# A hybrid attention block: the head norm's input is copied out of its bank by ScalarE, and scaled in SBUF by VectorE

## The chip, the core and the metric

One core of one Trainium2 chip runs the whole program. The metric is the device time of one launch in microseconds (us). The kernel before was timed in three runs: median 1075.9 us, lowest 1073.9, highest 1076.67. The execution that was profiled took 1073.98 us; its span, from the first instruction of the program to the last, is 1071.9 us, so 2.1 us lie around the span.

## The reference

One decoder layer over 512 real tokens and 16 meta tokens of width 1024, in float32: a SwiGLU feed-forward block, a token mixer with two attention branches and output gates, and a second feed-forward block. The change lies in the token mixer, where queries and keys of both branches pass through a norm over each head of 64 features:

```python
def rms_norm(x, g):
    xf = x.astype(jnp.float32)
    ms = jnp.mean(xf * xf, axis=-1, keepdims=True)
    return (xf * lax.rsqrt(ms + EPS) * g.astype(jnp.float32)).astype(x.dtype)

    proj = h @ w_in                       # h is the token's own rms_norm, 1024 wide
    qa = rms_norm(qa.reshape(b, p, FOX_HEADS, HEAD_DIM), fox_q_norm)
    ka = rms_norm(ka.reshape(b, p, FOX_HEADS, HEAD_DIM), fox_k_norm)
    ...
    qb = rms_norm(qb.reshape(b, p, SWA_Q_HEADS, HEAD_DIM), swa_q_norm)
    kb = rms_norm(kb.reshape(b, p, SWA_KV_HEADS, HEAD_DIM), swa_k_norm)
```

The forgetting branch (8 heads, all earlier tokens visible) and the sliding-window branch (8 query heads over 2 key heads, 128 tokens visible and the meta tokens) then compute scores, softmax and values.

## The kernel before

Every product runs as three fp32r products: each operand is split into a high part (`hi`, a copy on ScalarE, line 133 or 134) and a low part (`lo`, a subtraction on VectorE, line 140 or 142), and `prod` (lines 301, 302 and 304) multiplies high by high, high by low and low by high. Weights go the same way: the DMA lands in a tile `raw`, ScalarE writes `wh`, VectorE writes `wl`.

The mixer projects one tile of tokens at a time (128 tokens, or the 16 meta tokens, which are tile 0) against 256 columns of weights. `tok_chunk` makes two steps of each tile, with 12 matmuls each, and hands the finished bank to `evac`. For query and key columns `evac` calls `head_norm`: ScalarE squares the bank into a tile `hsq` (line 1057), VectorE sums each head into `hss` (line 1058) and applies the token's own mean square (`r1sq`, line 1059), and GpSimd raises it to the power -0.5 (line 351, in place). `head_norm` returns a function `scale`, which is called only when the next tile has been evacuated. It multiplies the bank by the token's factor `r1` and by the head's factor `hss` on VectorE (line 1073) and writes `qn`. So the bank of a tile is held from its first matmul until the scaling, one tile later. Tiles `qn` come from a pool of six. When all tiles of a chunk are there, `finish` transposes `qn` on TensorE (line 1153, 1161 or, for the sliding keys, 1407) and splits the result into `qH`, `qL`, `kH` and `kL`.

There are eight PSUM banks, four by the name `ps` and four by the name `pt`; in the mixer they are taken in turn, one of each name. All users share them: projections, transposes, scores and values.

The projection steps are woven between the steps of attention units (`weave`): a unit has `scores` (matmuls at line 1292, VectorE's addition and minimum at line 1310, exponentials at line 1209, normalisation at line 1212), `turn` (transposes at lines 1337 and 1350, split into `pH` and `pL`) and `values` (lines 1359, 1364 and 1365). A scheduler then sets the order of each engine's queue from the program order, the dependences and its own estimate of durations; this order is fixed when the program is built, and each engine works through its queue in that order. Scores of two heads use 64 of the 128 rows of TensorE each, one head the upper half and one the lower half, in a `ps` bank and a `pt` bank.

Of the kernel before, what the change touches and what calls it, by code (L numbers as in the profile page):

```python
# [13 lines left out]
AF = mybir.ActivationFunctionType  # L14
ALU = mybir.AluOpType
# [29 lines left out]
def bc(ap, pos, n):  # L45

    dims = [list(d) for d in ap.ap]
    dims.insert(pos, [0, n])
    return bass.AP(tensor=ap.tensor, offset=ap.offset, ap=dims)
# [33 lines left out]
def kernel(  # L83
# [22 lines left out]
    V, A, G, PE, SP = nc.vector, nc.scalar, nc.gpsimd, nc.tensor, nc.sync  # L106
# [9 lines left out]
    def nm(s):  # L116
        nid[0] += 1
        return f"{s}_{nid[0]}"
# [231 lines left out]
    def rsq(o, i):  # L350
        shared["pow"] = G.tensor_tensor(out=o, in0=i, in1=nhalf[: i.shape[0], : i.shape[1]], op=ALU.pow)
# [106 lines left out]
    class Units:  # L458
# [5 lines left out]
        def new(self, tag, bufs, w=1):  # L464
            return self.pool.tile([P, w * self.th], F32, tag=tag, name=nm(tag), bufs=bufs)
# [522 lines left out]
    r1 = cp.tile([P, NB + 1], F32, name="r1")  # L988
# [63 lines left out]
    def head_norm(ps, i, nh, outs):  # L1052

        n = M if i == 0 else P
        sq = new("hsq", [P, 256], F32, 3)
        ss = mp.tile([P, 4], F32, tag="hss", name=nm("hss"), bufs=4)[:n, :nh]
        A.activation(sq[:n, : nh * HD], ps[:n, : nh * HD], AF.Square)
        V.tensor_reduce(out=ss, in_=sq[:n, : nh * HD].rearrange("p (h d) -> p h d", d=HD), axis=AX.X, op=ALU.add)
        ts = V.tensor_scalar(ss, ss, r1sq[:n, i : i + 1], EPS, op0=ALU.mult, op1=ALU.add)
        shared["ts"] = getattr(ts, "ins", ts)  # L1060
        rsq(ss, ss)
        src, by = ps[:n, : nh * HD].rearrange("p (h d) -> p h d", d=HD), bc(ss, 2, HD)

        def scale():

            with tc.issue_after(shared["ts"]):
                r = r1[:n, i : i + 1]
                for o in outs:
                    a, b = src, by
                    if isinstance(o, tuple):  # L1070
                        o, par = o
                        a, b = (v.rearrange("p (a b) d -> p a b d", b=2)[:, :, par] for v in (src, by))
                    V.scalar_tensor_tensor(out=o, in0=a, scalar=r, in1=b, op0=ALU.mult, op1=ALU.mult)

        return scale

# [43 lines left out]
    def qk_chunk(box, tag, tiles, gcol):  # L1120
# [11 lines left out]
        def evac(i, ps):  # L1132
            n = M if i == 0 else P
            want = [0] if i == 0 else [i] if off else range(1, NB + 1)
            for j in want:
                if j not in qn:
                    qn[j] = new("qn", [P, 4, HD], F32, 6)
            if i == 0:
                G.memset(qn[i], 0.0)
            if off or i == 0:  # L1140
                return head_norm(ps, i, 4, [qn[i][:n]])
            pairs = lambda j: qn[j].rearrange("p (a b) d -> p a b d", b=2)
            return head_norm(ps, i, 4, [(pairs(i)[:, :, 0], 0), (pairs(NB + 1 - i)[:, :, 1], 1)])
# [231 lines left out]
    def kv_chunk(box):  # L1375
# [10 lines left out]
        def evac(i, ps):  # L1386
            n = M if i == 0 else P
            kd[i] = new("qn", [P, 2, 2, HD], F32, 6)
            if i == 0:
                G.memset(kd[i], 0.0)  # L1390
            scale = head_norm(ps, i, 2, [kd[i][:n, :, r] for r in range(2)])
            v_evac(box["v"][:, :, :256], i, ps[:n, P : 2 * P])
            return scale
# [140 lines left out]
    for i in every:  # L1534
        n = M if i == 0 else P
        ps = tok_result(ps0[i], i, 264)
        V.scalar_tensor_tensor(
            out=zf[:n, i], in0=ps[:, 256:264], scalar=r1[:n, i : i + 1], in1=fb[:n], op0=ALU.mult, op1=ALU.add
# [218 lines left out]
    src = {name: tuple([xS[name][:, p, k] for k in range(4)] for p in range(2)) for name in xS}  # L1757
# [78 lines left out]
    for i, step in enumerate(GATES):  # L1836
# [4 lines left out]
        b, m = step  # L1841
# [193 lines left out]
```

## Time and profile before

| what | value |
|---|---|
| median of three runs | 1075.9 us |
| profiled execution, its span | 1073.98 us, 1071.9 us |
| TensorE busy over the span | 1062.0 us (99%) |
| VectorE, ScalarE, GpSimd busy | 893.3 (83%), 652.8 (61%), 211.8 us (20%) |
| granted TensorE clock | 0.999 |
| scalings of line 1073 | 44, first at 386.9 us, last at 531.3 us |

In the rows, PE is TensorE, PEld its weight loads, DVE VectorE, ACT ScalarE, POOL GpSimd and SP SyncE. A row of grouped instructions gives line, engine, operation, output and inputs, shape, count, then busy us and mean ns of one, then the idle time of the engine just before them with what ended most of it. A row of the timeline gives start us, duration us, engine, line, operation, names, shape and count, and in brackets the idle time before it. Matmuls overlap, so the distance from one start to the next says more than a matmul's own duration.

### The profile page before, as it was taken

To read this page: it belongs to the slowest core of one execution; us is meant where nothing else is said; L and a number is where in the kernel's file an instruction comes from. 1 tells how busy PE (TensorE), PEld (TensorE's weight loads), DVE (VectorE), ACT (ScalarE), POOL (GpSimd) and SP (SyncE) were. 2 spreads that over 40 slices of the span, in tenths; PEclk is the share of its full clock that TensorE was granted. 3 is DMA by queue.
4 is the path that set the end of the run, shared out by engine and by line. 5 is a ranking of instruction groups with operands and counts; after the bars stand their busy time and mean duration, and the time that the engine had idled before them with its cause. 6 is when DMAs were issued, how large, how long until landed. Compare 5 with 4: busy or idle time off the path is not lost.

```text
span 1071.9 us, 22258 instructions
## 1 busy us (share of the span) xinstructions
PE 1062.0 (99%) x8515; PEld 1029.7 (96%) x8515; DVE 893.3 (83%) x1732; ACT 652.8 (61%) x1231; POOL 211.8 (20%) x281
## 2 busy tenths in 40 slices
PE   9999999999999999999999999999999999999998
PEld 8999999999999999999878799999999999999998
DVE  7988878888889678789897899888989788887895
ACT  7667456656666455556667776555665466745664
POOL 3011111121124432232200110001122211221120
PEclk9999999999999999999999999999999999999999
DMA  8787787688776413212311874566688877897763
GB/s 282 196 224 162 189 193 196 152 220 217 173 179 179 125 64 124 75 62 68 95 60 40 242 191 119 187 202 196 172 204 182 186 188 179 177 199 193 159 126 102
DMA packets 112571, 173.57 MB, mean 162 GB/s; under 512 B 10881, under 2 KB 59265, under 8 KB 112209
## 3 DMA queue, kind: packets, MB, share of 16 engines
q1 hardware_dynamic: 74464, 122.72, 36.4%
q0 software_dynamic: 29040, 37.83, 22.8%
q10 hardware_dynamic: 8960, 11.60, 3.3%
q8 instruction: 66, 1.08, 0.4%
q14 instruction: 41, 0.33, 0.1%
HBM read 167.89 MB, written 6.32 MB: 163 GB/s over the span
## 4 chain that ended last, share of the span: by engine, by line
PE 50%; DVE 3%; ACT 2%; issue 0%; DMA 0%; POOL 0%; ACTq 0%; DVEq 0%; POOLq 0%
PE ps L301 8%; PE ps L304 8%; PE ps L302 8%; PE pt L301 7%; PE pt L302 7%; PE pt L304 7%; ACT t L1209 1%; DVE wl L140 1%; ACT wh L133 1%; DVE pL L140 1%; PE ps L1473 0%; PE ps L1950 0%; PE pt L1473 0%; DMA raw<-in_wbr_dram 0%; DVE t L1212 0%
## 5 line engine op out<-in xcount | busy, mean ns | idle before, releaser
L301 PE MATMUL ps<-x,wh 128*128 128x256 f32 (+2 forms) x768 | 219.8, 286 | 0.2
L302 PE MATMUL ps<-x,wh 128*128 128x256 f32 (+2 forms) x768 | 218.9, 285 | 0.5 <-DVE x L142 0.4
L304 PE MATMUL ps<-x,wl 128*128 128x256 f32 (+2 forms) x768 | 218.8, 285 | 0.0
L140 DVE TENSOR_TENSOR wl<-raw,wh 128x1024 fp32r<-128x1024 f32 (+3 forms) x125 | 149.9, 1200 | 39.3 <-ACT wh L133 38.6
L133 ACT CAST wh<-raw 128x1024 fp32r<-128x1024 f32 (+3 forms) x125 | 128.4, 1029 | 85.7 <-PE ps L302 44.1
L301 PEld LDWEIGHTS ps<-x,wh 128*128 128x128 f32 x768 | 144.7, 189 | 1.8 <-ACT hT L686 0.3
L302 PEld LDWEIGHTS ps<-x,wh 128*128 128x128 f32 x768 | 144.5, 188 | 1.4 <-DVE x L142 0.9
L304 PEld LDWEIGHTS ps<-x,wl 128*128 128x128 f32 x768 | 144.7, 188 | 0.8
L301 PE MATMUL pt<-x,wh 128*128 128x256 f32 (+2 forms) x424 | 125.3, 296 | 0.0
L304 PE MATMUL pt<-x,wl 128*128 128x256 f32 (+2 forms) x424 | 124.6, 295 | 0.0
L302 PE MATMUL pt<-x,wh 128*128 128x256 f32 (+2 forms) x392 | 112.5, 287 | 0.0
L133 ACT CAST wh<-tc 128x1024 fp32r<-128x1024 f32 (+1 forms) x70 | 71.8, 1026 | 65.5 <-DVE tc L234 58.1
L140 DVE TENSOR_TENSOR wl<-tc,wh 128x1024 fp32r<-128x1024 f32 (+1 forms) x70 | 83.5, 1193 | 33.3 <-ACT wh L133 33.1
L301 PE MATMUL ps<-acts,wh 128*128 128x264 f32 (+1 forms) x352 | 100.5, 286 | 0.1
L304 PE MATMUL ps<-acts,wl 128*128 128x264 f32 (+1 forms) x352 | 99.8, 283 | 0.0
L302 PE MATMUL ps<-acts,wh 128*128 128x264 f32 (+1 forms) x352 | 99.6, 283 | 0.0
L140 DVE TENSOR_TENSOR wl<-rawC,wh 128x1024 fp32r<-128x1024 f32 (+1 forms) x70 | 84.2, 1202 | 5.7 <-ACT wh L133 5.2
L133 ACT CAST wh<-rawC 128x1024 fp32r<-128x1024 f32 (+1 forms) x70 | 71.5, 1022 | 22.8 <-PE pt L302 16.7
L301 PEld LDWEIGHTS pt<-x,wh 128*128 128x128 f32 x424 | 80.0, 189 | 2.3 <-ACT wh L133 0.2
L304 PEld LDWEIGHTS pt<-x,wl 128*128 128x128 f32 x424 | 79.8, 188 | 2.1
L302 PEld LDWEIGHTS pt<-x,wh 128*128 128x128 f32 x392 | 73.7, 188 | 0.6
L301 PEld LDWEIGHTS ps<-acts,wh 128*128 128x128 f32 x352 | 66.4, 189 | 0.7 <-DVE h2T L918 0.3
(446 smaller groups left out, 3236.5 us busy)
## 6 DMA issues: line engine op xcount, KB each, us to landing
rawC<-in_w1i_dram SPq DMA_DIRECT2D x20, 512.0 KB, 4.5
raw<-in_w1i_dram SPq DMA_DIRECT2D x40, 256.0 KB, 4.1
raw<-in_w2i_dram SPq DMA_DIRECT2D x40, 256.0 KB, 3.5
rawC<-in_w2i_dram SPq DMA_DIRECT2D x20, 512.0 KB, 4.3
raw<-in_wm_dram SPq DMA_DIRECT2D x18, 512.0 KB, 4.3
raw<-in_wout_dram SPq DMA_DIRECT2D x16, 512.0 KB, 4.0
rawD<-in_w1i_dram SPq DMA_DIRECT2D x20, 256.0 KB, 4.2
raw<-in_w1i_dram POOLq DMA_DIRECT2D x20, 256.0 KB, 5.4
```

The lines of the kernel that those rows point to most:

```text
L133: return A.copy(o, i)
L140: return V.tensor_tensor(out=o, in0=i, in1=h, op=ALU.subtract)
L301: PE.matmul(ps, sH, mH, start=first, stop=False, **more)
L302: PE.matmul(ps, sH, mL, start=False, stop=False, **more)
L304: shared["mm"] = PE.matmul(ps, sL, mH, start=False, stop=last, **more)
L1209: shared["exp"] = A.activation(t, t, AF.Exp, bias=nmx, scale=-1.0, accum_out=l[:, j : j + 1])
```

## The change

`head_norm` lets ScalarE copy the projected tile out of its bank, multiplied by the token's factor `r1`, right behind the square. The copy goes to the tile `qn` itself (for the sliding keys, to the first of its two places; for the forgetting keys, where the even and the odd heads go to two tiles, it is two copies of half the columns). `scale` then multiplies `qn` by the head's factor in place with a tensor-tensor operation; the second place of the sliding keys is written first, from the copy.

```diff
         src, by = ps[:n, : nh * HD].rearrange("p (h d) -> p h d", d=HD), bc(ss, 2, HD)
+        kept, todo = None, []
+        for o in outs:
+            a, b = src, by
+            if isinstance(o, tuple):
+                o, par = o
+                a, b = (v.rearrange("p (a b) d -> p a b d", b=2)[:, :, par] for v in (src, by))
+                kept = None
+            if kept is None:
+                kept = o
+                A.activation(kept, a, AF.Identity, scale=r1[:n, i : i + 1])
+            todo.append((o, kept, b))
 
         def scale():
 
             with tc.issue_after(shared["ts"]):
-                r = r1[:n, i : i + 1]
-                for o in outs:
-                    a, b = src, by
-                    if isinstance(o, tuple):
-                        o, par = o
-                        a, b = (v.rearrange("p (a b) d -> p a b d", b=2)[:, :, par] for v in (src, by))
-                    V.scalar_tensor_tensor(out=o, in0=a, scalar=r, in1=b, op0=ALU.mult, op1=ALU.mult)
+                for o, a, b in reversed(todo):
+                    V.tensor_tensor(out=o, in0=a, in1=b, op=ALU.mult)
```

The queues differ as follows. Line numbers behind line 1070 are six higher in the changed kernel.

ScalarE, in the first key chunk of the forgetting branch, behind the last load of an activation table; `hsq` is the square, `qn` the copy, `wh` the high part of a weight piece. Before:

```order
L1057 ACTIVATE hsq_5139<-ps_5110 128x256
L1057 ACTIVATE hsq_5171<-pt_5146 128x256
L1057 ACTIVATE hsq_5204<-ps_5179 128x256
L133 CAST wh_5076<-raw_4905 128x1024
L1057 ACTIVATE hsq_5237<-pt_5212 128x256
```

Now:

```order
L1057 ACTIVATE hsq_5140<-ps_5111 128x256
L1072 ACTIVATE qn_5136<-ps_5111,r_4883 128x2x64
L1072 ACTIVATE qn_5139<-ps_5111,r_4883 128x2x64
L1057 ACTIVATE hsq_5174<-pt_5149 128x256
L1072 ACTIVATE qn_5137<-pt_5149,r_4883 128x2x64
L1072 ACTIVATE qn_5138<-pt_5149,r_4883 128x2x64
L1057 ACTIVATE hsq_5209<-ps_5184 128x256
L1072 ACTIVATE qn_5138<-ps_5184,r_4883 128x2x64
L1072 ACTIVATE qn_5137<-ps_5184,r_4883 128x2x64
L133 CAST wh_5076<-raw_4905 128x1024
```

Each square is followed by its copies; the weight cast stands behind six of them.

TensorE, at the scores of an attention unit in the middle of the mixer, behind the transposes of the second key chunk (`kH`, `kL`, `qH` are split keys and queries; the 128x256 blocks of two heads go to a `ps` and a `pt` bank). Before:

```order
L1292 MATMUL ps_6171<-kH_5068,qH_5245 128x256
L1292 MATMUL ps_6179<-kH_5068,qH_5245 128x272
L1292 MATMUL ps_6179<-kL_5069,qH_5245 128x272
L1292 MATMUL ps_6179<-kH_5068,qH_5245 128x272
L301 MATMUL pt_6096<-wh_5759,x_4306 128x256
L302 MATMUL pt_6096<-wl_5760,x_4306 128x256
L304 MATMUL pt_6096<-wh_5759,x_4310 128x256
L301 MATMUL pt_6096<-wh_5759,x_4306 128x256
L1292 MATMUL pt_6172<-kH_5068,qH_5245 128x256
L1292 MATMUL pt_6172<-kL_5069,qH_5245 128x256
L1292 MATMUL pt_6172<-kH_5068,qH_5245 128x256
L302 MATMUL pt_6096<-wl_5760,x_4306 128x256
```

Now:

```order
L1167 MATMUL pt_6171<-ident,qn_5815 128x128 x2
L1298 MATMUL ps_6194<-kH_5068,qH_5254 128x256
L1298 MATMUL pt_6195<-kH_5068,qH_5254 128x256
L1298 MATMUL ps_6194<-kL_5069,qH_5254 128x256
L1298 MATMUL pt_6195<-kL_5069,qH_5254 128x256
L1298 MATMUL ps_6194<-kH_5068,qH_5254 128x256
L1298 MATMUL pt_6195<-kH_5068,qH_5254 128x256
```

The three matmuls of the second head no longer stand alone among projection matmuls; they alternate with those of the first head. The same happens once more, at the scores of the unit behind which the sliding keys are transposed.

TensorE, at the values of a later unit (`pv` is the `pt` bank, `pL` the low part of the probabilities). Before:

```order
L1364 MATMUL pt_6560<-pH_6530,v_4889 128x256
L301 MATMUL ps_6569<-wh_6043,x_4304 128x256
L302 MATMUL ps_6569<-wl_6044,x_4304 128x256
L304 MATMUL ps_6569<-wh_6043,x_4308 128x256
L301 MATMUL ps_6569<-wh_6043,x_4304 128x256
L302 MATMUL ps_6569<-wl_6044,x_4304 128x256
L1365 MATMUL pt_6560<-pL_6531,v_4889 128x256
```

Now:

```order
L1370 MATMUL pt_6589<-pH_6558,v_4889 128x256
L301 MATMUL ps_6598<-wh_6065,x_4304 128x256
L302 MATMUL ps_6598<-wl_6066,x_4304 128x256
L1371 MATMUL pt_6589<-pL_6559,v_4889 128x256
L1370 MATMUL pt_6589<-pH_6558,v_4889 128x128
L1371 MATMUL pt_6589<-pL_6559,v_4889 128x128
L304 MATMUL ps_6598<-wh_6065,x_4308 128x256
```

The matmul that reads `pL` stands three projection matmuls further forward. At two later units it stands one further forward, at an earlier unit two, and at one unit three further back.

## The prediction

> **What bounds the kernel now.** I read three views first: busy time by engine, then two stretches of 160 us side by side (a piece of the feed-forward block, and the piece of the mixer in which all 44 scalings lie), then the waits of TensorE. Columns of the stretches are length, busy us of PE, PEld, DVE, ACT and POOL with counts, granted clock, DMA share, GB/s.
>
> ```profile
> PE 1062.0 (99%) x8515; PEld 1029.7 (96%) x8515; DVE 893.3 (83%) x1732; ACT 652.8 (61%) x1231; POOL 211.8 (20%) x281
> ```
>
> ```profile
> 100.00:260.00 160.00, 159.98 (x1313) 159.66 (x1312) 131.45 (x221) 90.68 (x155) 29.38 (x34) 1.00 0.80 194
> 380.00:540.00 160.00, 157.38 (x1291) 147.40 (x1290) 131.37 (x392) 94.77 (x227) 46.91 (x92) 1.00 0.26 81
> 480.00:500.00 20.00, 19.76 (x168) 18.66 (x169) 18.45 (x61) 13.10 (x37) 4.81 (x13) 1.00 0.30 83
> ```
>
> ```profile
> PE pt L1365 <- DVE pL L140: 0.9, 3, 0.4
> PE ps L1292 <- DVE qn L1073: 0.5, 1, 0.5
> ...
> PE pt L1350 <- DVE qn L1073: 0.2, 1, 0.2
> ```
>
> TensorE is busy 99% of the span, at full clock. In the feed-forward stretch it idles for 0.02 us of 160; in the mixer stretch for 160 - 157.38 = 2.62 us. That is the whole reservoir of waits that this edit can empty, apart from matmuls that could stand better. 0.3% of 1075.9 us, about what a measurement of this kernel can tell from no change, is 3.2 us. VectorE is the engine that TensorE waits for: it is busy 82% of the mixer stretch and 18.45 of the worst 20 us, and the waits name its `pL` and its `qn`. ScalarE is busy 59% there, but the split of the probabilities, the exponentials and the weight casts all pass through it.
>
> **What the edit removes and adds.** The view of line 1073 counts the scalings, and the groups of the mixer give durations:
>
> ```profile
> L1073 DVE SCALAR_TENSOR_TENSOR qn<-ps,r,hss x22: 333/349/483, 388.3 to 531.3; 128x128 f32<-128x128 f32 x12, 128x256 f32<-128x256 f32 x10
> L1073 DVE SCALAR_TENSOR_TENSOR qn<-pt,r,hss x18: 332/347/484, 389.4 to 528.3; 128x128 f32<-128x128 f32 x12, 128x256 f32<-128x256 f32 x6
> L1073 DVE SCALAR_TENSOR_TENSOR qn<-hsq,r,hss x4: 332/399/473, 386.9 to 476.0; 16x256 f32<-16x256 f32 x2, 16x128 f32<-16x128 f32 x2
> ```
>
> ```profile
> L1106 DVE TENSOR_TENSOR oA<-pt,hsq 64x256 f32<-64x256 f32 x20 | 8.4, 420 | 2.2 <-ACT hsq L1105 1.8
> L1073 DVE SCALAR_TENSOR_TENSOR qn<-ps,r,hss 128x256 f32<-128x256 f32 x10 | 4.7, 474 | 0.0
> L1736 DVE SCALAR_TENSOR_TENSOR spare<-xg,gT,spare 128x256 f32<-128x256 f32 x4 | 1.7, 479 | 0.0
> ```
>
> The new operation, a tensor-tensor of 256 columns, has its nearest row in `oA`: 420 ns. The old one took 474, and the same operation with all its tensors in SBUF took 479. So leaving the bank gains VectorE nothing by itself; losing the scalar operand gains 0.05 to 0.06 us. 44 x 0.06 = 2.6 us of VectorE over the stretch. The bounds are 0 (no gain) and 2.6 us. Where it counts is ahead of a late `pL`: the view of waits has three at line 1365, and two scalings stand shortly before such a `pL` in VectorE's queue. I take **0.4 us** (3 x 2 x 0.06).
>
> [...]
>
> ScalarE gains 39 copies: 16 of 256 columns (queries), 20 of 128 (16 forgetting keys, 4 sliding keys), 3 of the meta tile.
>
> ```profile
> L134 ACT ACTIVATE v<-pt,r 128x256 fp32r<-128x256 f32 x5 | 2.4, 471 | 0.0
> ...
> L134 ACT ACTIVATE v<-ps,r 128x128 fp32r<-128x128 f32 x2 | 0.7, 362 | 0.0
> ```
>
> ```profile
> 491.52 0.38 ACT L1057 ACTIVATE hsq<-ps 128x256 f32<-128x256 f32 x1 [0.58 <-PE ps L304]
> 491.80 0.37 ACT L133 CAST pH<-ps 128x256 fp32r<-128x256 f32 x1
> ```
>
> The `v` rows are the same operation with the same scalar, 0.47 and 0.36 us. From the two timeline rows, the next instruction starts 0.10 us before the end of the last (491.80 against 491.90), so a copy holds up its queue by 0.37 or 0.26 us: 16 x 0.37 + 20 x 0.26 + 3 x 0.35 = **12.2 us** of ScalarE. This is the price of the edit, and the bounds are 0 and 12.2 us. Behind a copy stand, by turns, a probability cast (as at 491.80), a weight cast, an exponential or the next square. ScalarE idles 65 of the 160 us, and in the changed queue the exponentials and one probability cast stand ahead of the square that they followed. The cover is this idle time; where it is gone, `pH` is late, then `pL`, then line 1365. A copy waits for what its square has waited for (and for a free `qn`, whose transposes stand more than a tile earlier). I take **0.5 us**: two sites where a copy stands straight before a late cast.
>
> **What the bank's release gives.** Two waits name the scaling although the waiting matmul reads no `qn`: scores at line 1292 and probabilities at line 1350. They wait for the bank.
>
> ```profile
> 435.86 0.35 PE L1292 MATMUL ps<-kH,qH 64*128 64x256 f32 x1 [0.55 <-DVE qn L1073]
> ```
>
> ```profile
> 480.09 0.52 PE L1350 MATMUL pt<-ident,t 128*128 128x128 f32 x3 [0.24 <-DVE qn L1073]
> ```
>
> The copy releases the bank a tile earlier, so both go: **0.8 us** (0.55 + 0.24). What is late next there is VectorE's own `pL` and `t`, which are not in these rows; the bounds are 0 and 0.8.
>
> **What the moved matmuls give.** Scores of two heads that alternate run side by side; alone, each set of three pays for itself and for both changes of shape.
>
> ```profile
> 481.37 0.38 PE L1292 MATMUL ps<-kH,qH 64*128 64x256 f32 x1
> 481.37 0.38 PE L1292 MATMUL pt<-kH,qH 64*128 64x256 f32 x1
> ...
> 482.30 0.39 PE L301 MATMUL ps<-wh,x 128*128 128x256 f32 x1
> ```
>
> ```profile
> 452.04 0.28 PE L301 MATMUL pt<-wh,x 128*128 128x256 f32 x1
> 452.25 0.38 PE L1292 MATMUL pt<-kH,qH 64*128 64x256 f32 x1
> 452.47 0.28 PE L1292 MATMUL pt<-kL,qH 64*128 64x256 f32 x1
> 452.59 0.27 PE L1292 MATMUL pt<-kH,qH 64*128 64x256 f32 x1
> 452.79 0.39 PE L302 MATMUL pt<-wl,x 128*128 128x256 f32 x1
> ```
>
> ```profile
> 495.73 0.38 PE L1292 MATMUL ps<-kH,qH 64*128 64x256 f32 x1
> ...
> 496.28 0.44 PE L1407 MATMUL pt<-ident,qn 128*128 128x128 f32 x2
> ```
>
> Both heads start together at 481.37, and twelve matmuls are through in 0.93 us. The lone set at 452.25 stretches the step from one projection matmul to the next from 0.12 (452.47 to 452.59 shows the step of such a stream) to 0.75 us: 0.63 lost. The lone set at 495.73 costs 0.55. In the new order both run inside their partner's time. I take **1.1 us**; bounds 0, if the second bank is still late and the pair waits together, and 1.2.
>
> Against it stand the matmuls on `pL` that come further forward.
>
> ```profile
> 477.16 0.39 PE L1365 MATMUL pt<-pL,v 128*128 128x256 f32 x1 [0.31 <-DVE pL L140]
> ```
>
> This one already waits for VectorE, and three projection matmuls of 0.12 us now stand behind it: 0.36 us more. Two others stand one matmul further forward, 0.12 each at most. **0.6 us** lost in all; the bounds are 0, where VectorE is early enough, and 0.6. The one that moves back and the earlier one that moves forward I count at nothing: the three waits of that row are elsewhere.
>
> **Sum.** -0.4 - 0.8 - 1.1 + 0.5 + 0.6 = **-1.2 us**. Against the profiled execution's own 1073.98 us (its span of 1071.9 and 2.1 around it) that is 1072.8; that execution was 1.9 us under the median, so as a median I forecast 1075.9 - 1.2 = **1074.7 us**, no measurable change.
>
> **The rivals.**
>
> *ScalarE's queue gets in the way (slower).* Place: the probability casts and exponentials in 430 to 535 us, where a copy is queued ahead of them. The other terms give -1.7 us without the 0.5. So the kernel is slower by over 3.2 us if 4.9 of the 12.2 us, 40%, reach TensorE; at half (6.1) the time is 1075.9 - 1.7 + 6.1 = 1080.3. For it: each `pL` and `wl` of VectorE needs ScalarE's half first. Against it: ScalarE idles 41%, the square at 491.52 had 0.58 us of idle time ahead of it, and the waits quoted name VectorE alone. Chance 0.12.
>
> *The two-input scaling collides with GpSimd.* The scaling now reads two tensors in SBUF while GpSimd raises `hss` to its power there.
>
> ```profile
> L351 POOL TENSOR_TENSOR hss<-hss,nhalf 128x4 f32<-128x4 f32 x24 | 25.9, 1080 | 41.4 <-DVE hss L1059 41.4
> ```
>
> GpSimd is busy 46.91 of 160 us, 29%. If a scaling that meets it waits for half a power (0.54 us), that is 44 x 0.29 x 0.54 = 6.9 us of VectorE. A third of it on the path would be 2.3 us: 1077.0; all of it, 1081.6. Against it: VectorE's weight split has both inputs in SBUF too, and in the mixer, where GpSimd is busier (46.91 against 29.38), it took only 1236 ns against 1200 over the program:
>
> ```profile
> L140 DVE TENSOR_TENSOR wl<-raw,wh 128x1024 fp32r<-128x1024 f32 x29 | 35.9, 1236 | 4.0 <-ACT wh L133 4.0
> ```
>
> ```profile
> L140 DVE TENSOR_TENSOR wl<-raw,wh 128x1024 fp32r<-128x1024 f32 (+3 forms) x125 | 149.9, 1200 | 39.3 <-ACT wh L133 38.6
> ```
>
> Chance 0.05. [...]
>
> *The banks were the hidden limit (faster).* If the early release takes away all of the mixer's idle time, 2.6 us, with the 1.1 us of paired scores and half of the 0.4, the time is 1075.9 - 3.9 = 1072.0. For it: eight banks shared by all. Against it: only 0.8 us of the waits name the scaling. Chance 0.15.
>
> *Nothing moves.* The released banks wait for the next late thing, and the pairs run no earlier: 1075.9. Chance 0.10.
>
> **How the numbers follow.** My forecast has 0.58. Of it 0.56 lies within 0.3% and 0.02 below. The first rival is slower with all its 0.12; the second gives 0.02 to slower and 0.03 to the same; the third 0.13 to faster and 0.02 to the same; the last 0.09 to the same and 0.01 to slower. Faster 0.15, same 0.70, slower 0.15. The range reaches down to all gains at their bounds (2.6 + 0.8 + 1.2 - 0.6 = 4.0 us, with no copy on the path) less 0.7 us for the spread of a median, 1071.2, and up to a third of the copies' 12.2 us on the path (1075.9 - 1.7 + 4.1), 1078.3.
>
> **What would show it.** Right: the waits of lines 1292 and 1350 for `qn` are gone; the new tensor-tensor takes 0.41 to 0.43 us at 256 columns and the copies 0.46 to 0.48; twelve matmuls at line 1298 alternate where three stood alone; TensorE's idle time in the mixer stretch falls from 2.6 to about 1.8 us, with the wait at 477 us grown. Wrong: new waits of TensorE for `pH`, or for `pL` behind a ScalarE that was never idle; a tensor-tensor of over 0.5 us; or a bank that stays late although the copy is done, because something else holds it.

## The result, and the profile after

In 22 runs each, the changed kernel takes **1073.66 us** (1072.82 to 1075.08) and the kernel before 1075.23 us (1073.9 to 1077.24): a ratio of 0.9986, with a 95% interval of 0.9981 to 0.9992. The change gains 1.57 us, 0.15%. The forecast was -1.2 us and 1074.7 us.

The profiled execution of the changed kernel has a span of 1071.2 us (before 1071.9). First the busy time by engine, then the same 160 us of the mixer as before, with the same columns, then the waits of TensorE in the mixer (total us, times, longest).

```profile
PE 1060.0 (99%) x8515; PEld 1028.1 (96%) x8515; DVE 891.8 (83%) x1732; ACT 666.4 (62%) x1270; POOL 212.9 (20%) x281
```

```profile
380.00:540.00 160.00, 156.93 (x1299) 147.46 (x1298) 131.32 (x394) 107.57 (x268) 47.89 (x92) 1.00 0.26 81
```

```profile
PE pt L1371 <- DVE pL L140: 1.6, 4, 0.7
PE ps L1370 <- ACT pH L133: 0.3, 1, 0.3
PE ps L1413 <- DVE nmx L1316: 0.3, 1, 0.3
PE ps L1159 <- DVE qn L1079: 0.3, 1, 0.3
PE ps L302 <- DVE wl L140: 0.2, 1, 0.2
```

(Lines behind the edit are six higher than before: 1371 was 1365, 1298 was 1292.) The two waits for the bank are gone. In their place stand more waits for `pL`, and one each for `pH`, `nmx`, the transposes' `qn` and a weight piece `wl`. TensorE idles 160 - 156.93 = 3.07 us in this window, more than the 2.62 before, and yet eight more matmuls lie in it.

The operations came out close to the rows that stood for them. The groups of the mixer, shapes apart:

```profile
L1079 DVE TENSOR_TENSOR qn<-qn,hss 128x256 f32<-128x256 f32 x16 | 6.7, 418 | 2.0 <-POOL hss L351 2.0
L1079 DVE TENSOR_TENSOR qn<-qn,hss 128x128 f32<-128x128 f32 x24 | 6.2, 285 | 0.4 <-POOL hss L351 0.3
L1072 ACT ACTIVATE qn<-ps,r 128x256 f32<-128x256 f32 x10 | 4.7, 470 | 0.0
L1072 ACT ACTIVATE qn<-ps,r 128x128 f32<-128x128 f32 x10 | 3.3, 377 | 0.0
```

**Where the time went.** Busy shares don't answer that here, so I made a ledger: the matmuls of each trace are numbered by their start, 8515 in each kernel, and the start of the same number is compared with that in the kernel before. The difference at the mixer's first scalings (389 us) is taken off, since it is -0.58 to +1.31 us in these profiles and arises in the first block, where the kernels are alike. What is left is the gain (-) or loss (+) of each stretch, in us; the stretches are named by the times of the kernel before. Each ledger rests on one profile, and inside a group of matmuls whose order has changed the same number can be another matmul. But a step with the same cause comes out alike: nine of the kernels below and here have -0.90 or -0.92 us at 433 to 437 us.

| kernel | 389-433 | 433-437 | 437-448 | 448-457 | 457-476 | 476-487 | 487-494 | 494-497 | 497-507 | 507-518 | 518-531 | 531-562 | sum |
|---|---|---|---|---|---|---|---|---|---|---|---|---|---|
| changed | -0.05 | -0.90 | +0.07 | -1.08 | +0.24 | -0.38 | +0.25 | -0.23 | +0.54 | +0.50 | +0.01 | -0.29 | -1.32 |

So the change wins 2.9 us in five places and gives 1.6 us back in five others. The wins come first (436 to 482 us); most of the losses come at 490 to 515 us.

### The profile page after: what moved, and what is told of

The parts are those of the page before. It is cut to its first block, busy times and chain, and to the rows that moved or that the text cites. A ratio compares the mean times of both kernels' runs of the same rounds, so it can differ in the third digit from the quotient of the medians.

```text
span 1071.2 us, 22299 instructions
## 1 busy us (share of the span) xinstructions
PE 1060.0 (99%) x8515; PEld 1028.1 (96%) x8515; DVE 891.8 (83%) x1732; ACT 666.4 (62%) x1270; POOL 212.9 (20%) x281
## 3 DMA queue, kind: packets, MB, share of 16 engines
q8 instruction: 66, 1.08, 0.4%
## 4 chain that ended last, share of the span: by engine, by line
PE 49%; DVE 2%; ACT 2%; issue 0%; ACTq 0%; POOL 0%; DVEq 0%; POOLq 0%
PE ps L301 8%; PE ps L304 8%; PE ps L302 8%; PE pt L301 7%; PE pt L302 7%; PE pt L304 7%; ACT t L1215 1%; PE ps L1479 1%; DVE wl L140 0%; PE ps L1956 0%; PE pt L1479 0%; ACT wh L133 0%; DVE pL L140 0%; PE pt L1494 0%; PE pt L1496 0%
```

## The experiments

All kernels compute the whole layer. In each the scheduler orders the queues anew, so an edit also moves some instructions that it doesn't name. Each was timed in 11 runs beside 33 of the kernel before on the same chip, whose median was 1075.29, 1074.95 and 1074.67 us in the three sets of four. The intervals are about 0.9 us to each side, so the ledger says more of a place than the time does of the whole. By their times 6, 7 and 9 to 12 are faster than the kernel before and 5 is slower; 1, 2, 3, 4 and 8 cannot be told from it. The theory under test is the prediction's own sum; rivals are named in each expectation. The ledgers of all experiments, columns as above:

| kernel | 389-433 | 433-437 | 437-448 | 448-457 | 457-476 | 476-487 | 487-494 | 494-497 | 497-507 | 507-518 | 518-531 | 531-562 | sum |
|---|---|---|---|---|---|---|---|---|---|---|---|---|---|
| 1 lighter operation only | -0.30 | -0.12 | 0 | 0 | +0.01 | +0.04 | +0.10 | +0.33 | +0.01 | +0.07 | -0.12 | +0.77 | +0.78 |
| 2 the same, not in the sliding queries | -0.42 | -0.12 | -0.02 | +0.02 | -0.02 | +0.05 | +0.11 | +0.32 | 0 | -0.01 | 0 | +0.01 | -0.08 |
| 3 copies only | +0.42 | 0 | -0.13 | 0 | +0.11 | +0.04 | -0.05 | +0.24 | -0.01 | +0.30 | -0.01 | +0.04 | +0.94 |
| 4 release, old operation | +0.53 | -0.90 | +0.61 | -1.08 | +0.33 | -0.41 | +0.34 | -0.22 | +0.53 | +0.59 | +0.01 | -0.08 | +0.25 |
| 5 copies twice | +2.22 | -0.90 | +0.27 | -1.09 | +0.19 | -0.38 | +0.36 | -0.22 | +0.68 | +0.75 | +0.01 | -0.16 | +1.72 |
| 6 plain copies | +0.30 | -0.90 | -0.12 | -1.08 | +0.25 | -0.39 | +0.36 | -0.23 | +0.46 | +0.39 | -0.01 | -0.28 | -1.26 |
| 7 heads one after the other | +0.27 | -0.90 | -0.01 | -1.09 | +0.24 | -0.40 | +0.12 | -0.01 | +0.47 | +0.33 | +0.18 | -0.33 | -1.12 |
| 8 halves one after the other | +0.91 | 0 | -0.01 | -1.08 | +1.04 | -0.39 | -0.02 | +0.25 | +0.52 | -0.64 | +0.18 | -0.35 | +0.40 |
| 9 copies in second keys, queries | +0.03 | -0.90 | +0.07 | -1.08 | +0.24 | +0.06 | +0.03 | 0 | 0 | +0.01 | -0.01 | 0 | -1.56 |
| 10 and in sliding keys | +0.04 | -0.90 | +0.06 | -1.08 | +0.24 | -0.42 | +0.27 | 0 | -0.08 | +0.05 | 0 | +0.03 | -1.80 |
| 11 all but sliding queries | -0.02 | -0.92 | +0.07 | -1.08 | +0.24 | -0.40 | +0.23 | 0 | -0.06 | +0.01 | 0 | +0.01 | -1.92 |
| 12 as 11, plain copies | +0.29 | -0.90 | -0.12 | -1.08 | +0.27 | -0.42 | +0.36 | 0 | -0.03 | +0.02 | +0.01 | -0.01 | -1.61 |

### 1. The lighter operation without copies

```diff
-    V.tensor_scalar(r1sq, r1sq, 1.0 / HD, None, op0=ALU.mult)
+    V.reciprocal(r1sq, r1sq)
+    V.tensor_scalar(r1sq, r1sq, EPS, None, op0=ALU.mult)
...
-    ts = V.tensor_scalar(ss, ss, r1sq[:n, i : i + 1], EPS, op0=ALU.mult, op1=ALU.add)
+    ts = V.tensor_scalar(ss, ss, 1.0 / HD, r1sq[:n, i : i + 1], op0=ALU.mult, op1=ALU.add)
...
-    V.scalar_tensor_tensor(out=o, in0=a, scalar=r, in1=b, op0=ALU.mult, op1=ALU.mult)
+    V.tensor_tensor(out=o, in0=a, in1=b, op=ALU.mult)
```

> The scaling stays in the bank and no copy is made, but it becomes a tensor-tensor: the token's factor is folded into the head's factor (the constant under the root is divided by the square of the token's factor). Only the term for the lighter operation is left. My prediction's term: -0.4 us, so 0.4 us under the kernel before, with the scaling at about 420 ns for 256 columns, and the two bank waits of 0.55 and 0.24 us still there. Theory B, the released banks do all of the gain: no change at all, and the bank waits unchanged. Theory L, the lighter operation does it: the whole 1.5 us that the change gave.

Measured: 1076.09 us against 1075.29, ratio 1.0009 (1.0 to 1.0018). None of the three forecasts has a loss in it. The operation does fall from 474 to 418 ns in the bank, and the bank waits stay, as expected:

```profile
L1073 DVE TENSOR_TENSOR qn<-ps,hss 128x256 f32<-128x256 f32 x10 | 4.2, 418 | 1.6 <-POOL hss L351 1.5
```

The ledger first shows the gain, -0.42 us up to 437 us, and then two losses, 0.33 us at 495 and 0.77 at 534. The second, in the timeline (start, duration, then the instruction, in brackets the idle time before it):

```profile
529.67 0.42 DVE L1073 TENSOR_TENSOR qn<-ps,hss 128x256 f32<-128x256 f32 x1 [0.73 <-POOL hss L351]
530.01 1.22 DVE L140 TENSOR_TENSOR wl<-raw,wh 128x1024 fp32r<-128x1024 f32 x1
...
535.95 0.30 PE L1473 MATMUL ps<-ident,t 128*128 128x128 f32 x1 [1.05 <-DVE t L1212]
```

In this kernel the scheduler has put this scaling ahead of a weight split (in the kernel before it stood three instructions behind that split, at 531.30 us). There it waits 0.73 us for GpSimd's power with all of VectorE's queue behind it, and 6 us later TensorE waits 1.05 us where it waited 0.27 us. The operation itself is faster; its new place in the queue is what costs.

### 2. The lighter operation, but not in the sliding queries

Edit: as in 1, with the folded factor for all chunks but `qb0` and `qb1`, which keep the old operation and its factor.

> The lighter operation alone, in the bank and without copies, but not for the sliding queries, whose scaling keeps the old operation. The run with the lighter operation everywhere lost 0.33 us at 495 and 0.77 us at 534 us, after VectorE's queue had been put in another order; both lie in the sliding queries' stretch. Theory Q, the lighter operation by itself gains my 0.4 us and only the changed order of the queue took it back: the two losses go, and the kernel is 0.2 to 0.5 us under the kernel before. Theory B, with the bank held the lighter operation gains nothing: within 0.2 us of the kernel before or slower.

Measured: 1075.62 us against 1074.67, ratio 1.0007 (0.9998 to 1.0016); the ledger's sum is -0.08 us, so the time itself settles nothing. By the ledger theory Q is half right: the 0.77 us at 534 us are gone, the 0.32 at 495 are not. There the scaling is late and the scores wait for its bank:

```profile
488.92 1.21 DVE L140 TENSOR_TENSOR wl<-raw,wh 128x1024 fp32r<-128x1024 f32 x1
490.05 0.68 DVE L140 TENSOR_TENSOR pL<-ps,pH 128x512 fp32r<-128x512 f32 x1
...
492.03 0.36 ACT L1127 COPY hsq<-pt 64x256 f32<-64x256 f32 x1 [2.85 <-PE pt L1387]
492.42 0.43 DVE L1128 TENSOR_TENSOR oA<-pt,hsq 64x256 f32<-64x256 f32 x1 [1.23 <-ACT hsq L1127]
...
494.39 0.48 DVE L1091 TENSOR_TENSOR qn<-ps,hss 128x128 f32<-128x128 f32 x2
...
494.51 0.28 PE L1314 MATMUL pt<-kH,qH 64*128 64x272 f32 x1
494.93 0.39 PE L1314 MATMUL ps<-kH,qH 64*128 64x272 f32 x1
```

`oA` (the sum of an attention unit's values) stands ahead of the sum of squares in both kernels. Here a weight split (488.92) has come ahead of the subtraction that makes `pL`, which in the kernel before stood first. So the matmuls on `pL` (line 1387) are later, then ScalarE's copy of their bank, and `oA` waits 1.23 us for that copy. The scaling behind it ends at 494.87 and the `ps` matmul starts at 494.93, after 0.42 us in which the stream's step is 0.12. As long as VectorE frees the bank, a delay further up VectorE's queue can reach TensorE.

### 3. The copies without the release

The scaling still reads the bank and overwrites what the copy wrote.

```diff
+    kept = None
+    for o in outs:
+        ...
+            A.activation(kept, a, AF.Identity, scale=r1[:n, i : i + 1])
     def scale():
         ...
```

> The kernel before with the 39 scaled copies added into the same tiles, while the scaling still reads the bank and overwrites them: the price of the copies without the release. My prediction's term: +0.5 us, with ScalarE some 14 us busier and the bank waits still there. The rival with ScalarE's queue in the way: over 40% of 12.2 us, +4.9 us or more, with waits of TensorE for pH behind a never idle ScalarE. Theory F, the copies are free: within 0.2 us of the kernel before.

Measured: 1075.92 us against 1075.29, ratio 1.0008 (0.9999 to 1.0017), +0.63 us; the ledger has +0.94. By the time the forecast term of +0.5 us holds, by the ledger it was nearly double; the rival of 4.9 us is out. That the copies are free (theory F) is against the ledger, but the time alone, whose interval begins at -0.1 us, doesn't exclude it. The price is not spread: 0.39 us lie at one place, 391 us, another 0.54 at 495 and 512 us, and the other stretches add up to nothing.

### 4. The release with the old operation

```diff
-                for o, a, b in reversed(todo):
-                    V.tensor_tensor(out=o, in0=a, in1=b, op=ALU.mult)
+                r = ones[:n, 0:1]
+                for o, a, b in reversed(todo):
+                    V.scalar_tensor_tensor(out=o, in0=a, scalar=r, in1=b, op0=ALU.mult, op1=ALU.mult)
```

> The changed kernel with the old, heavier operation: the copy releases the bank, the scaling in SBUF is a scalar-tensor-tensor again (its scalar is a column of ones). By my sum without the 0.4 us: -0.8 - 1.1 + 0.5 + 0.6 = -0.8 us against the kernel before, the operation at 474 to 479 ns for 256 columns, the bank waits gone. Theory B, the banks do it all: -1.5 us as the change itself. Theory L, the lighter operation does it: no gain, 0 to +0.5 us. Should VectorE gain by leaving the bank, the operation would come out well under 474 ns.

Measured: 1075.45 us against 1075.29, ratio 1.0003 (0.9994 to 1.0012). The operation takes as long in SBUF as it took in the bank, 477 ns against 474:

```profile
L1080 DVE SCALAR_TENSOR_TENSOR qn<-qn,ones,hss 128x256 f32<-128x256 f32 x16 | 7.6, 477 | 2.0 <-POOL hss L351 2.0
```

The wins of the release are all there (-0.90, -1.08, -0.41, -0.22), and still the sum is +0.25 where the changed kernel has -1.32. The lighter operation, with the few places in the queues that change along with it, is worth 1.57 us here, much more than the 0.4 of my sum. 0.44 us of them lie at 391 to 394 us, where the weights are late, and 0.54 at 446 us, where something else happens as well:

```profile
442.37 0.60 DVE L1080 SCALAR_TENSOR_TENSOR qn<-qn,ones,hss 128x128 f32<-128x128 f32 x2
442.54 2.44 POOL L351 TENSOR_TENSOR hss<-hss,nhalf 128x4 f32<-128x4 f32 x1 [2.44 <-DVE hss L1059]
442.90 1.22 DVE L140 TENSOR_TENSOR wl<-raw,wh 128x1024 fp32r<-128x1024 f32 x1
...
445.02 0.63 DVE L1080 SCALAR_TENSOR_TENSOR qn<-qn,ones,hss 128x128 f32<-128x128 f32 x2 [0.31 <-POOL hss L351]
445.57 0.54 DVE L140 TENSOR_TENSOR pL<-ps,pH 128x384 fp32r<-128x384 f32 x1
...
446.17 0.39 PE L1372 MATMUL ps<-pL,v 128*128 128x256 f32 x1 [0.59 <-DVE pL L140]
```

A power of GpSimd takes 2.44 us, where the mean in the kernel before is 1.08. It begins under a scaling with a weight split right behind it and ends 0.86 us after that split; the next power is late, then the next scaling, then `pL`, then TensorE. How much of the 0.54 us is this and how much the heavier operation, one run doesn't tell.

### 5. Each copy twice

```diff
+                A.activation(kept, a, AF.Identity, scale=r1[:n, i : i + 1])
                 A.activation(kept, a, AF.Identity, scale=r1[:n, i : i + 1])
```

> The changed kernel with each copy issued twice into the same tile: ScalarE pays another 12.2 us of its queue, and the bank is released one copy later. By my term a further +0.5 us over the changed kernel, and not more than 1.0. The rival with ScalarE's queue in the way: +4.9 us or more over the changed kernel. Theory F, the copies are free: within 0.2 us of the changed kernel.

Measured: 1076.80 us against 1075.29, ratio 1.0018 (1.0009 to 1.0027). The ledger is 3.0 us worse than the changed kernel's, between my 0.5 to 1.0 and the rival's 4.9. 1.9 of the 3.0 us are lost at one place, in the first chunk:

```profile
390.96 0.37 ACT L1073 ACTIVATE qn<-ps,r 128x128 f32<-128x128 f32 x1
391.23 1.03 ACT L133 CAST wh<-raw 128x1024 fp32r<-128x1024 f32 x1
...
392.30 1.23 DVE L140 TENSOR_TENSOR wl<-raw,wh 128x1024 fp32r<-128x1024 f32 x1 [1.17 <-ACT wh L133]
392.32 0.39 PE L301 MATMUL ps<-wh,x 128*128 128x256 f32 x1 [0.94 <-ACT wh L133]
...
393.58 0.39 PE L302 MATMUL ps<-wl,x 128*128 128x256 f32 x1 [0.87 <-DVE wl L140]
```

Squares and copies of the first tiles stand ahead of the next weights' cast, and the weights come late. Everywhere else together the second set of copies costs 1.1 us more.

### 6. Plain copies

Edit: the changed kernel with the folded factor of experiment 1 and `A.copy(kept, a)` for the scaled copy.

> The changed kernel with the token's factor folded into the head's factor, so that the copy needs no factor and is a plain copy. If the factor is what makes the copy dearer than a cast of its size (0.47 against 0.37 us at 256 columns), the copies fall to about 0.37 us and ScalarE gains some 3 us; by my term (0.5 for 12.2 us) that is worth 0.1 us, by theory S about half of the losses at 393 and 500 us, 0.2 to 0.3 us. The scaling should keep its 418 ns. If the copy stays at 0.47 us, the time stays that of the changed kernel.

Measured: 1073.28 us against 1074.95, ratio 0.9988 (0.9979 to 0.9996). The copies fall as expected:

```profile
L1073 ACT COPY qn<-ps 128x256 f32<-128x256 f32 x10 | 3.7, 366 | 0.0
L1073 ACT COPY qn<-ps 128x128 f32<-128x128 f32 x10 | 2.3, 285 | 0.0
```

The scaled copy costs 470 - 366 = 104 ns more than the plain one at 256 columns and 377 - 285 = 92 at 128; the operation changes along with the factor. The shorter copy buys little: 0.19 us at 446 us and 0.19 at 500 and 512 us, and 0.36 us are lost at 417 us, where the transposes now wait 0.5 us for `t`. Against the changed kernel no difference can be told.

### 7. and 8. What pairing is worth

Experiment 7 writes the three score matmuls of one head before those of the other; 8 writes all sets of one head (two or three) before all of the other and ties them in that order (the comments are added here):

```diff
-    for qx, kx in ((0, 0), (0, 1), (1, 0)):
-        for hb, ps, spans in zip(half, two, block):       # before: in turn
+    for hb, ps, spans in zip(half, two, block):           # 7: three and three
+        for qx, kx in ((0, 0), (0, 1), (1, 0)):
...
+    for hh in range(2):                                   # 8: six or nine, then six or nine
+        for b, block in enumerate(blocks):
+            i = 2 * ip + b
+            for pi in range(len(block[0])):
...
+                with tc.issue_after(getattr(last, "ins", last)) if last is not None else ExitStack():
```

> The changed kernel with the score matmuls written one head after the other instead of in turn: 20 pairs of triples, most of which then stand alone. This measures the disputed price of a lone triple. By my row (twelve alternating matmuls in 0.93 us, a lone triple 0.55 to 0.63 us) each pair that comes apart costs some 0.3 us on TensorE, 4 to 6 us over all. The rival, alternation is worth nothing because matmuls of one half follow each other as fast as those of two: within 0.5 us of the changed kernel.

> The changed kernel with the score matmuls of a unit queued in another order: first all sets of the one head (two or three sets of three), then all of the other, tied in that order. Head by head in single sets, the two halves of TensorE still started together in the trace (434.38 and 434.39 us) although three matmuls stood between them in the queue. Theory N, TensorE starts the other half's matmul ahead of at most some three that are queued before it: now six or nine stand between, most sets run alone, and 18 pairs at 0.3 to 0.36 us cost 5 to 6 us. Theory W, the two halves have queues of their own and run side by side however the sets are ordered, so only a full-height matmul between them parts them: within 0.5 us of the changed kernel, and the halves still start together.

Measured: 7 takes 1073.36 us against 1074.95, ratio 0.9983 (0.9974 to 0.9992), as fast as the changed kernel. So my 4 to 6 us fell, and the trace says why. In 7 three `pt` matmuls stand in TensorE's queue ahead of the `ps` ones:

```profile
434.38 0.45 PE L1298 MATMUL pt<-kH,qH 64*128 64x400 f32 x1
434.39 0.45 PE L1298 MATMUL ps<-kH,qH 64*128 64x400 f32 x1
434.67 0.34 PE L1298 MATMUL pt<-kL,qH 64*128 64x400 f32 x1
434.68 0.34 PE L1298 MATMUL ps<-kL,qH 64*128 64x400 f32 x1
```

By these records the fourth matmul of the queue started with the first. Nothing came apart. In 8 nine `pt` matmuls stand ahead:

```profile
435.39 0.45 PE L1303 MATMUL pt<-kH,qH 64*128 64x400 f32 x1
...
436.31 0.28 PE L1303 MATMUL pt<-kH,qH 64*128 64x272 f32 x1
436.32 0.45 PE L1303 MATMUL ps<-kH,qH 64*128 64x400 f32 x1
436.43 0.27 PE L1303 MATMUL pt<-kH,qH 64*128 64x256 f32 x1
```

Here the first `ps` matmul starts with the sixth `pt` one, again three places ahead of its turn: theory N's reach. Three matmuls of the first half start after it, at 436.43, 436.55 and 436.67. The kernel takes 1075.22 us against 1074.67, ratio 1.0007 (0.9998 to 1.0016), and the units at 412 and 419, 434 and 471 us lose 0.64, 0.90 and 0.80 us against experiment 7. If of three sets two come to run alone, and of two sets one, that is 0.2 to 0.45 us for each, about the 0.3 expected. But the sum is 1.5 us and not 5 to 6: fewer sets come apart than the 18 I counted, TensorE's waits for `pL` fall from 1.5 us in experiment 7 to 0.4, and at 507 to 518 us the ledger gains 0.97 us against it: what TensorE loses on itself it no longer waits for there.

```profile
380.00:540.00 160.00, 158.75 (x1292) 150.51 (x1290) 129.97 (x391) 107.45 (x267) 48.54 (x92) 1.00 0.26 81
```

TensorE idles 1.25 us in this window, less than in any other kernel here, and the kernel is no faster than the one before.

### 9. to 11. Copies in some of the chunks

9 copies in the second keys and second queries, 10 in the sliding keys as well, 11 in all chunks but the sliding queries (the comments are added here):

```diff
-    def head_norm(ps, i, nh, outs):
+    def head_norm(ps, i, nh, outs, copied=True):       # False: scaled in the bank, as before
...
-    ka = qk_chunk(f0, "k", every, 1)
+    ka = qk_chunk(f0, "k", every, 1, False)            # 9, 10; True in 11
```

> Copies and released banks for the second keys and second queries alone. Theory S: the gains of 436 us (0.83) and 450 to 457 us (1.1) belong to these two chunks, those of 474 and 482 us (0.65) to the sliding keys, whose release also costs 0.25 us at 491: 1.6 to 2.0 us under the kernel before, some 0.2 to 0.4 us above the run that copies the sliding keys too. The rival, the gains of 474 to 482 us come along from the earlier ones: no difference from that run.

> Copies and released banks only in the three middle chunks (second keys, second queries, sliding keys); the first keys and queries and both chunks of sliding queries are scaled in the bank as before. Theory S, the price sits where a copy stands ahead of a late weight cast (393 us) or a late probability cast (500 us) and in the matmuls that the early release lets come forward too far, and the gain sits at 436 to 482 us, in the middle chunks: the gains of 436 to 482 us stay (2.0 to 2.7 us), the losses of 393 and 500 us go, so 1.8 to 2.5 us under the kernel before and 0.3 to 0.9 under the changed kernel. Theory A, all chunks release banks to one common gain: less copies give less, between the two kernels (0.5 to 1.2 us under the kernel before).

> The changed kernel without the copies of the sliding queries alone (their scaling in the bank as before); the first chunks are copied. Theory S: as the changed kernel up to about 490 us, then without its loss of 0.6 us at 500 us and of 0.5 at 512: 0.5 to 1.0 us under the changed kernel. Theory A: slower than the changed kernel by what the sliding queries gave, 0.3 to 0.5 us.

Measured: 9 takes 1073.19 us against 1074.67, ratio 0.9989 (0.9980 to 0.9998); 10 takes 1072.85 against 1074.95, 0.9981 (0.9972 to 0.9990); 11 takes 1072.51 against 1074.95, 0.9979 (0.9971 to 0.9988). Theory S holds in its places, if not in every size: 9 gains a little less than its 1.6 to 2.0 us (1.48 by the time, 1.56 by the ledger), and 10 had no loss at 391 us to win back, since the changed kernel has none there on balance (-0.05). The wins at 436 and 450 to 457 us belong to the second keys and queries, since 9 has them alone. The win at 480 us (-0.4) and the loss at 490 (+0.25) belong to the sliding keys. The losses at 500 and 512 us, 1.0 us together, belong to the sliding queries, whose release wins 0.5 us at 495 and 536. Without it, 11 is the best kernel of the study, 0.6 us under the changed one by the ledger. (By the times their intervals overlap.)

### 12. The best one with plain copies

Edit: experiment 11 with the folded factor and `A.copy` in the copied chunks.

> The best kernel so far (copies in all chunks but the sliding queries, 1072.5 us) with the token's factor folded into the head's factor for the copied chunks, so that their copies are plain ones (0.10 us shorter each, as measured). Theory S: the remaining losses at 393 and 446 us (0.13 each) go, 0.1 to 0.3 us under that kernel. The rival, a changed order of a queue costs more than that: 0.2 to 0.6 us over it.

Measured: 1073.46 us against 1074.67, ratio 0.9988 (0.9979 to 0.9997). The rival holds in its sign and, against 11 by the ledger, at 0.3 us in its size: 0.19 us are won at 446 us, and 0.44 lost before 433 us (a wait for `t`, as in 6) and at 490. Plain copies are no improvement.

## Why the prediction was right, and where it was not

The forecast, -1.2 us, came within 0.4 us of the median's -1.57 and 0.1 of the ledger's -1.32. The steps behind it were less right than their sum: each gain was larger than I took it, and so were the losses, in other places. The sum had 2.3 us of gains and 1.1 of losses, the ledger has 2.9 and 1.6. That the difference fits so well is in part luck.

**Bank waits, taken as -0.8.** The mechanism was right: each wait left in every kernel that releases its bank and in none that doesn't (1, 2 and 3 keep both, 9 keeps the second). The sizes were too small: at these two waits the ledger steps by 0.90 and 0.41 us, where the brackets said 0.55 and 0.24. A bracket counts from the end of the last matmul, some 0.28 us after its start, while in an undisturbed stream the next starts 0.12 us after it (451.80 and 451.92 in the kernel before). The time that a wait costs is read from start to start.

**Score matmuls, taken as -1.1.** -1.08 us at 448 to 457 and -0.23 at 495, where the sum had 0.63 and 0.55; that the two together come so near is luck. At the first site the kernel before had the transposes of line 1161 (450.53) in the middle of the first head's sets, which I had not counted, and now they stand ahead; on the other hand one set of the second head still stands alone (451.28 in the changed kernel). At the second site the sets pair as forecast, but the transposes behind them now wait:

```profile
494.48 0.33 PE L1413 MATMUL ps<-ident,qn 128*128 128x128 f32 x1 [0.31 <-DVE nmx L1316]
```

They read no `nmx`, so it is a bank that they wait for. One part of the step was wrong: the halves do not have to alternate in the queue (7). What parted them was a full-height matmul between them (in the kernel before the second head's set, queued behind four of these, started at 452.25, after the last of the four at 452.04), or more than three of the same half (8).

**The lighter operation, taken as -0.4.** Alone it won 0.54 us up to 437 us (2) and lost nearly all of that again, most of it at 495 us, where the bank is still held. With the bank released it was worth 1.57 us (4 against the change), some of it by way of one long power of GpSimd. So neither half of the edit gains by itself: the ledger has +0.78 or -0.08 us for the operation (1, 2), +0.25 for the release (4) and -1.32 for both. The step mis-sized was "3 x 2 x 0.06": I counted only the scalings shortly ahead of the three waits that the trace showed. VectorE's queue counts at more places: against the change, 4 loses at 391 to 394, 446 and 534 us as well. That the release uncovers these places is my reading; no run shows it by itself. Leaving the bank was worth nothing by itself, as forecast: the old operation took 474 ns in the bank (the kernel before) and 477 in SBUF (4), the new one 418 in the bank (1) and 418 in SBUF (the changed kernel).

**Copies, taken as +0.5.** +0.94 by the ledger without the release (3), nearly double. In the changed kernel a clear case is at 499 us. The timeline there:

```profile
498.50 0.39 ACT L1057 ACTIVATE hsq<-ps 128x256 f32<-128x256 f32 x1
...
498.78 0.47 ACT L1072 ACTIVATE qn<-ps,r 128x256 f32<-128x256 f32 x1
...
499.14 0.48 ACT L133 CAST pH<-ps 128x384 fp32r<-128x384 f32 x1
...
499.67 0.38 PE L1370 MATMUL ps<-pH,v 128*128 128x256 f32 x1 [0.32 <-ACT pH L133]
```

A copy stands straight before a late probability cast and holds it up by 0.36 us, as the prediction had described such a site. But in 3 the same stretch costs nothing, so the copy is not enough: here the matmuls on this `pH` also stand further forward (next paragraph). No run has the moved matmuls without the copy.

**Moved matmuls, taken as +0.6.** The named place was wrong. At 477 us of the kernel before hardly anything was lost; in the changed kernel the wait there is 0.35 us at 475.72, against 0.31. The losses came at 488, 500 and 512 us, +1.3 us with the copy's part:

```profile
487.97 0.39 PE L1371 MATMUL pt<-pL,v 128*128 128x256 f32 x1 [0.39 <-DVE pL L140]
...
512.46 0.38 PE L1371 MATMUL pt<-pL,v 128*128 128x256 f32 x1 [0.72 <-DVE pL L140]
```

At 488 (+0.25) the matmul on `pL` is one of the two that stand one place forward, taken as 0.12 at most. At 500 (+0.54) it is the unit whose matmul on `pL` moves back by three, which I counted at nothing: by the number of their start its first two matmuls on `pH` stand four places further forward, and the second of them waits (499.67 above). At 512 (+0.50) nothing has moved: the matmul has the same number in both kernels. A copy (508.74) stands ahead of a weight cast there, and VectorE's split and `pL` come behind it; in 3 this place costs 0.30 us without the release. I had read the changed order at the places where the kernel before waits, and counted the rest at nothing.

**Not in the sum:** +0.24 us at 466 to 471 (transposes wait for `qn`), and -0.3 at 536 (a wait for `t`, 0.27 us before, gone).

**The rivals.** ScalarE's queue in the way: the price without the release is 0.6 to 0.9 us (3), far from 4.9; at double the copies it comes to 3 (5). GpSimd's collision with the scaling: the scaling keeps its 418 ns in the bank and in SBUF, so it does not show there. Banks as the hidden limit: partly true, for they passed on more than their waits named; but the idle time did not fall. That was the part of "what would show it" that failed: idle time from 2.6 to 1.8 us was forecast, 3.07 came. And one of its signs of being wrong came too, a new wait for `pH` (499.67), at one place and with 0.32 us.

Five profiles (1, 3, 4, 5, 6) show a further loss of 0.3 to 0.5 us at 623 us, past the mixer (10 has 0.2), in a wait of TensorE for ScalarE at the second feed-forward block. It bears no relation to the copies (1 has none), and I did not follow it. Nor was the first block's 1.9 us of spread from profile to profile.

## What to carry to other kernels

A buffer that is released earlier wins where something waits for it and costs where the released work runs ahead of its data; where both happen in one kernel, release it only for the work whose release wins (here the second keys, the second queries and the sliding keys, three of seven chunks; the first keys and queries make 0.1 us between 10 and 11). When the bottleneck engine is 99% busy, compare the start of the same numbered instruction in both traces: its idle time went up in the better kernel and down to its least in a worse one. And an edit of 0.06 us in a scheduled queue can lengthen a wait by 0.8 us (experiment 1): read the new order of the queue before reading the duration.

## What the runs showed of the hardware

TensorE started a matmul of one half of its rows up to three places ahead of its turn in the queue, past matmuls of the other half (434.39 us in experiment 7, 436.32 in 8). So by these records of starts TensorE does not work through its queue strictly in order, and the time of experiment 7 agrees: at 1073.36 us it lost nothing to the changed kernel's 1073.66.

GpSimd's power over four heads of 128 tokens, 1.01 to 1.28 us elsewhere in the kernel before, took 2.30 us once there and 2.44 us once in experiment 4, both times with a weight split of VectorE right behind a scaling; in experiment 1 one took 2.25 us (511.19). The one in the kernel before:

```profile
510.87 0.47 DVE L1073 SCALAR_TENSOR_TENSOR qn<-pt,r,hss 128x256 f32<-128x256 f32 x1
511.04 2.30 POOL L351 TENSOR_TENSOR hss<-hss,nhalf 128x4 f32<-128x4 f32 x1 [2.32 <-DVE hss L1059]
511.26 1.21 DVE L140 TENSOR_TENSOR wl<-raw,wh 128x1024 fp32r<-128x1024 f32 x1
```

It ended 0.87 us after the split (513.34 against 512.47), that of experiment 4 0.86 us after its own (444.98 against 444.12). By the starts the power was first (511.04 against 511.26), yet it was the power that took long: the split took 1.21 us, no longer than the mean of 1236 ns in the prediction's row of such splits. And in the changed kernel a power at 390.36 us with a split 0.23 us behind took 1.18 us, so what decides is open.
